# The down stage of a hybrid layer: two pairs interleaved product by product in each chunk, six weight parts split ahead, larger activation loads, and row sums spread over four blocks

## The chip, the core and the metric

The kernel runs on one core of a Trainium2 chip. The core has five engines with an instruction queue each: TensorE (PE in the profile; its weight loads are listed apart as PEld), VectorE (DVE), ScalarE (ACT), GpSimd (POOL) and SyncE (SP), which here only issues transfers. ACT also issues some. An engine runs its queue in order, so an instruction that waits holds up all that stands behind it. The metric is the device time of one execution in microseconds (us), the median over runs. A change of 0.2%, or 5 us, is about what a measurement of this kernel can tell from none.

## What is computed

One layer of a streaming encoder over 17 tiles of 128 rows (16 tiles of a prompt, one of samples), width 1024, in float32. It begins with a norm, an input projection, a gated delta rule beside a short convolution, and an output projection; the change leaves these alone. The second half, which it touches, is the feed-forward part:

```python
    h = rmsnorm(x, norm_ffn_pre)
    f = (jax.nn.silu(h @ w_gate) * (h @ w_up)) @ w_down
    x = x + rmsnorm(f, norm_ffn_post)
```

`w_gate` and `w_up` are 1024 x 2816, `w_down` is 2816 x 1024. The last line is the last norm; its result is the output `out_y`.

## The kernel before, in words

**Split products.** Each float32 factor is split into a high part (a cast by ACT) and the rest (a subtraction on VectorE or GpSimd), and a product is three matmuls: high x high, high x low, low x high. So each operand of a matmul costs a cast and a subtraction first, and a matmul that finds its operand not yet split waits. Around these stand forms with seven products in the place of eight: sums of blocks of the factors are formed first ("parts"), and the seven results are added into four sums.

**Gate and up stage (1123 to 2025 us).** The 17 tiles form three groups of 6, 6 and 5 tiles (`FGROUPS`). Each group goes through 22 blocks f of 128 columns (the matmuls of L1268, seven products per block, in `gate_up`). Of group 0, a block takes 14.5 us. In a block ACT copies PSUM banks out (L1300 to L1302), VectorE and GpSimd add them up, ACT applies SiLU (L1311, L1316), and VectorE multiplies. Next to that the weights of the next block are summed (`s` tiles sA to sD, L1234 to L1237) and split (L1243, L1244). Results are stored to DRAM in the layout in which the down stage reads them: `partd` for pairs of row blocks, `lastd` for the row block that is left single (stores L1332, L1340 and L1342, issued by ACT). At f = 16 of groups 0 and 1 the row sums of the next group are formed on VectorE: twelve subtractions, four each of L1166, L1167 and L1169 (`ffn_sums`).

**Down stage (2025.6 to 2492 us).** The 22 blocks form five chunks (`FCHUNKS`) of 4, 4, 4, 4 and 6 blocks. Per chunk there are c = 2 (in the last c = 3) slices q, and 7 x c weight parts, numbered (i, q); a part is a pair of 128 x 512 tiles `dw` (high and low), which `part` makes out of the rows that L1092 loads: a sum on VectorE for i = 1, 2, 3, 5 (L1099 to L1105), a cast on ACT (L1116) and a subtraction on VectorE or GpSimd (L1118). The parts live in a ring of 21 slots. Some slots reuse tiles of the stage before (sA and sB). `prep_step` makes the next part; five parts of the first chunk are made during blocks 11 to 15 of the last group, with the first two activation parts.

Eight pairs and one single run through every chunk. A pair is seven products with 3 x c matmuls of 128 x 512 each (L1434; 42 in a chunk with c = 2, 63 in the last); its seven activation parts are loaded by SP (L1424) in three loads of 2, 2 and 3 parts, and split by ACT (L1415) and VectorE or GpSimd (L1418, tile `as`). Four PSUM banks take the products of a pair; each is added into the accumulators `acc` by VectorE (L1393; in the first chunk ACT copies, L1467). Products 4 to 6 use banks that products 0 to 2 filled, so they wait until these were taken out. The pairs run one after the other, the single after the first pair (in the last chunk at the end). In the last chunk a pair ends with its last norm: two subtractions (L1493, L1494) and, for each of its two row blocks in `finish`, two squares on ACT (L1443), a sum (L1444), `f2m` on VectorE (L145), the power on GpSimd (L147), two products with `gpo` (L1447) and two multiply-adds (L1452) on VectorE, and two stores of `out_y`, one issued by ACT and one by SP.

**What sets the order.** The code names which engine does what; the order in which each engine's queue holds its instructions comes from a scheduler that simulates the program, within waits that the tiles' buffers and the `issue_after` marks set. So an edit can move instructions that it does not name, and the order is shown below where it matters.

## Time and profile before

| | us |
|---|---|
| median of 3 runs | 2511.01 |
| lowest and highest run | 2507.51, 2511.68 |
| profiled execution, its own time | 2506.84 |
| span in its trace | 2505.1 |
| TensorE busy, of the span | 2455.0 |
| end of the gate and up stage, begin of the down stage | 2025.6 |
| last matmul ends | 2492.5 |

The last two rows are from the timeline. Between span and time of the profiled execution lie 1.7 us. A row of the profile's groups reads: line, engine, operation, output <- inputs (names of tiles), shapes, count | busy us, mean ns of one | idle time before, and what ended it. A row of the waits reads: engine, what it was to write, line <- whom it waited for: us in all, times, longest. In the table by windows each engine has its busy time and in brackets the number of instructions, then the granted TensorE clock, and the share of the DMA engines and GB/s. A timeline row is: start, duration, engine, line, operation; a row with xN covers N instructions.

### The profile page before, as it was taken

Reading aid. Unit: us, or ns where it says so; the run is one execution under the profiler, and the core shown is the slowest. Engines: PE = TensorE matmul, PEld = TensorE weight load, DVE = VectorE, ACT = ScalarE, POOL = GpSimd, SP = SyncE. Lnnn points to the kernel's source line nnn. Section 1 sums busy time; section 2 is a strip of 40 time slices with the busy share of each in tenths; the row PEclk is TensorE's granted clock in tenths of the full one; section 3 lists DMA queues with packets and bytes.
Section 4 is the critical chain, followed back from the end, with each engine's and each line's share of the span. In section 5 each row is a group of like instructions: output and inputs, shape, how many; then the busy total and the mean of one; then the engine's idle time right before and its main releaser. Section 6 shows DMA issues by size and latency. Waiting matters only on the chain. (4 is left out here: it accounts for less than half of the span.)

```text
span 2505.1 us, 39369 instructions
## 1 busy us (share of the span) xinstructions
PE 2455.0 (98%) x14366; PEld 2247.2 (90%) x14366; DVE 1610.7 (64%) x3032; ACT 1059.6 (42%) x2355; POOL 579.5 (23%) x656
## 2 busy tenths in 40 slices
PE   8999999999999999999999999999999999999997
PEld 7898888889999988889999999999999987887786
DVE  5976645645656555878888754455555564677698
ACT  5556445445435343444443422223333345333343
POOL 1101011011011001135665400000000055455563
PEclk9999999999999999999999999999999999999999
DMA  7855555456667556688876878778898843333365
GB/s 275 310 213 193 211 198 193 175 170 231 242 225 240 200 183 211 209 297 319 292 269 238 290 250 277 264 242 267 291 308 280 259 147 122 93 126 126 128 224 184
DMA packets 282499, 561.91 MB, mean 224 GB/s; under 512 B 26109, under 2 KB 174785, under 8 KB 265025
## 3 DMA queue, kind: packets, MB, share of 16 engines
q1 hardware_dynamic: 161200, 483.52, 56.1%
q10 hardware_dynamic: 121104, 75.88, 9.7%
q8 instruction: 113, 1.85, 0.3%
q14 instruction: 82, 0.66, 0.1%
HBM read 400.62 MB, written 158.70 MB: 223 GB/s over the span
## 5 line engine op out<-in xcount | busy, mean ns | idle before, releaser
L1268 PE MATMUL fbank<-xh,fw 128*128 128x384 f32 (+1 forms) x3696 | 897.8, 326 | 5.9 <-ACT m L1300 2.6
L298 PE MATMUL dbank<-hi,w 128*128 128x384 f32 (+1 forms) x2240 | 672.0, 368 | 8.8 <-ACT w L277 6.2
L1268 PEld LDWEIGHTS fbank<-xh,fw 128*128 128x128 f32 x3696 | 651.0, 188 | 7.5 <-ACT m L1300 3.0
L1268 PE MATMUL fbank<-xl,fw 128*128 128x384 f32 (+1 forms) x1848 | 601.9, 326 | 0.0
L298 PEld LDWEIGHTS dbank<-hi,w 128*128 128x128 f32 x2240 | 416.8, 190 | 47.8 <-ACT w L277 6.2
L1434 PE MATMUL fbank<-dw,as 128*128 128x512 f32 x1884 | 442.6, 393 | 7.5 <-DVE as L1418 2.6
L1434 PEld LDWEIGHTS fbank<-dw,as 128*128 128x128 f32 x1884 | 353.6, 188 | 90.3 <-DVE acc L1393 3.9
L298 PE MATMUL dbank<-lo,w 128*128 128x384 f32 (+1 forms) x1120 | 402.3, 359 | 1.1 <-DVE lo L216 1.1
L1268 PEld LDWEIGHTS fbank<-xl,fw 128*128 128x128 f32 x1848 | 346.9, 188 | 0.0
L1418 POOL TENSOR_TENSOR as<-ar,as 128x256 fp32r<-128x256 f32 (+1 forms) x207 | 186.8, 913 | 226.3 <-ACT as L1415 223.8
L298 PEld LDWEIGHTS dbank<-lo,w 128*128 128x128 f32 x1120 | 212.9, 190 | 18.7 <-DVE lo L216 1.7
L1393 DVE TENSOR_TENSOR acc<-acc,fbank 128x512 f32<-128x512 f32 x248 | 166.3, 682 | 96.1 <-PE fbank L1434 81.9
L1415 ACT CAST as<-ar 128x256 fp32r<-128x256 f32 (+1 forms) x288 | 118.5, 428 | 184.6 <-PE fbank L1434 133.9
L1118 POOL TENSOR_TENSOR dw<-dr,dw 128x512 fp32r<-128x512 f32 x48 | 70.0, 1467 | 520.3 <-ACT dw L1116 520.3
L1243 ACT CAST fw<-rg 128x512 fp32r<-128x512 f32 x124 | 77.4, 624 | 193.8 <-PE fbank L1268 153.1
L302 DVE SCALAR_TENSOR_TENSOR acc<-R,cw,acc 128x384 f32<-128x384 f32 (+2 forms) x180 | 121.6, 678 | 53.2 <-ACT acc L332 44.2
L1313 DVE TENSOR_TENSOR c<-u,fbank 128x384 f32<-128x384 f32 (+1 forms) x66 | 34.9, 529 | 109.9 <-PE fbank L1268 109.9
L1311 ACT ACTIVATE m<-fbank 128x384 f32<-128x384 f32 (+1 forms) x66 | 31.3, 474 | 124.4 <-PE fbank L1268 117.3
L1309 DVE TENSOR_TENSOR m<-m,m 128x384 f32<-128x384 f32 (+1 forms) x44 | 23.1, 525 | 88.8 <-ACT m L1302 88.7
L1244 POOL TENSOR_TENSOR fw<-rg,fw 128x512 fp32r<-128x512 f32 x44 | 71.0, 1614 | 37.0 <-ACT fw L1243 34.7
L324 POOL COPY hist<-R 128x3 f32<-128x3 f32 x60 | 17.0, 283 | 254.5 <-ACT R L307 201.9
L1302 ACT COPY m<-fbank 128x384 f32<-128x384 f32 (+1 forms) x66 | 30.6, 463 | 82.9 <-PE fbank L1268 57.8
(362 smaller groups left out, 3550.6 us busy)
## 6 DMA issues: line engine op xcount, KB each, us to landing
w<-wsplit SPq DMA_DIRECT2D x105, 1024.0 KB, 5.1
fw<-fsplit SPq DMA_DIRECT2D x188, 512.0 KB, 4.7
fsplit<-fw SPq DMA_DIRECT2D x94, 512.0 KB, 3.9
partd<-pt ACTq DMA_DIRECT2D x88, 384.0 KB, 6.6
rg<-in_w_gu SPq DMA_DIRECT2D x62, 512.0 KB, 3.8
wsplit<-w SPq DMA_DIRECT2D x28, 1024.0 KB, 4.9
ar<-partd SPq DMA_DIRECT2D x48, 384.0 KB, 3.3
wr<-in_w_in SPq DMA_DIRECT2D x34, 512.0 KB, 5.8
```

Source lines behind the costliest of these rows:

```text
L298: T.matmul(ps[:, :c], l[:, k, :], r[k][:, :c], start=(k == 0 and r is hi and l is wh), stop=(k == KD - 1 and l is wl))
L302: r = V.scalar_tensor_tensor(acc, raw(d), w[:, d:d + 1], acc, op0=ALU.mult, op1=ALU.add)
L1118: e.tensor_tensor(out=w[1], in0=v, in1=w[0].bitcast(F32), op=ALU.subtract)
L1243: A.copy(w[:, 0], v)
L1244: e.tensor_tensor(out=w[:, 1], in0=v, in1=w[:, 0].bitcast(F32), op=ALU.subtract)
L1268: T.matmul(ps, w_[:, c], b_[k][:, :hw], start=(first and k == 0 and ci == 0), stop=(k == KH - 1 and ci == 2), skip_group_check=not first)
L1311: A.activation(sg0, b1, AF.Silu)
L1313: V.tensor_add(c21, u2, b3)
L1393: V.tensor_add(dst, dst, ps)
L1415: ins = A.copy(a[:, 0, :n], v)
L1418: e.tensor_tensor(out=a[:, 1, :n], in0=v, in1=a[:, 0, :n].bitcast(F32), op=ALU.subtract)
L1434: T.matmul(ps, a[:, x_, q * P:(q + 1) * P], w[y_], start=(start and q == 0 and ci == 0), stop=(q == c - 1 and ci == 2), skip_group_check=True)
```

## The change

Its parts, in the order of the kernel:

1. In `ffn_sums` the twelve subtractions are no longer formed at f = 16 together, but three per block at f = 16, 17, 18 and 19. For group 0 the tiles T3 now live in the tiles sA to sD, all four of which lie in one pool.
2. Six weight parts of the first down chunk are made ahead in the place of five, in blocks 10 to 15; the sixth slot lies in sC and sD.
3. In every down chunk, pairs 0 and 1 run as a "duo": their products alternate (in the first chunk in the order A, A, B, B and then by turns, since A has two activation parts ready; afterwards A, B, A, B). A weight part is now used by two products in a row. The single runs after the duo. In the last chunk the last norms of both pairs follow the duo's last product.
4. For the duo, activation parts are loaded in larger pieces: parts 2 to 6 at once for the first pair of the first chunk, 0 to 3 and 4 to 6 for the others. In the first chunk all seven splits of the second pair are on VectorE (before: two of seven).
5. `gpo` is loaded at the third chunk in the code's order and no longer at the second. Both halves of `out_y` are stored by SP, apart from the last ones.
6. In the very last norm the products with `gpo` go into a tile of their own, `xm`, and stand in the code beside the squares; the two accumulators of the single are two tiles.

Line numbers of the changed kernel differ: L1435 is the matmul of the down stage, L1473 the copy out of the banks in the first chunk, L1446 the squares, L1448 and L1453 the products with `gpo`, L1449 the sum, L1458 the multiply-add, L1460 the store, L1510 and L1511 the two subtractions.

```diff
@@ -1106,10 +1106,10 @@
             m = n % NDW
-            if m == NDR:
-                w = [ks.tile([P, 512], F32R, tag=nm, name=nm) for nm in SUMS[:2]]
+            if NDR <= m < NDR + 2:
+                w = [ks.tile([P, 512], F32R, tag=nm, name=nm) for nm in SUMS[2 * (m - NDR):2 * (m - NDR) + 2]]
             else:
-                pool, b = (dr, NDR) if m < NDR else (da, NDQ) if m <= NDR + NDQ else (dn, NDW - NDR - 1 - NDQ)
+                pool, b = (dr, NDR) if m < NDR else (da, NDQ) if m < NDR + 2 + NDQ else (dn, NDW - NDR - 2 - NDQ)
@@ -1157,10 +1157,10 @@
 
-        def ffn_sums(gi, hs, fs):
+        def ffn_sums(gi, hs, fs, sums=None, ks=range(KH)):
             hw = len(FGROUPS[gi]) * P // 2
-            t3, t2 = [], []
-            for k in range(KH):
+            t3, t2 = sums or ([], [])
+            for k in ks:
@@ -1177,7 +1177,7 @@
                     if nm == "T3" and not sums:
-                        t3.append(fs.tile([P, HW], F32, tag="t3", name="ft3", bufs=KH)[:, :hw])
+                        t3.append(ks.tile([P, 512], F32R, tag=SUMS[k], name="ft3").bitcast(F32)[:, :hw])
@@ -1230,7 +1230,7 @@
                 wl[:] = [nc.sync.dma_start(out=ru, in_=w_gu[f, 1].rearrange("p k c -> p (k c)"))]
-                s = [(fe if q > 1 else ks).tile([P, 512], F32R, tag=nm, name=nm).bitcast(F32) for q, nm in enumerate(SUMS)]
+                s = [ks.tile([P, 512], F32R, tag=nm, name=nm).bitcast(F32) for nm in SUMS]
@@ -1358,9 +1358,9 @@
                             hs.append(next(hload))
-                    if f == NF - 6:
+                    if NF - 6 <= f < NF - 6 + KH:
                         with tc.issue_after(gmark["V"].ins):
-                            t3 = ffn_sums(gi + 1, hs, fd)
+                            t3 = ffn_sums(gi + 1, hs, fd, t3 if f > NF - 6 else None, [f - NF + 6])
@@ -1378,7 +1378,7 @@
                     prep_step(1)
-                elif 11 <= f < 12 + NDR:
+                elif 10 <= f < 12 + NDR:
@@ -1420,9 +1420,10 @@
             n = src.shape[-2] * P
-            a = da.tile([P, 4, MC * P // 2], F32, tag="ar", name="ar", bufs=3)
-            nc.sync.dma_start(out=a[:, :hi - lo, :n], in_=src[:, lo:hi].rearrange("p i q c -> p i (q c)"))
-            return [a[:, i, :n] for i in range(hi - lo)]
+            a = da.tile([P, 4 * MC * P // 2], F32, tag="ar", name="ar", bufs=3)
+            a = a[:, :(hi - lo) * n].rearrange("p (i c) -> p i c", c=n)
+            nc.sync.dma_start(out=a, in_=src[:, lo:hi].rearrange("p i q c -> p i (q c)"))
+            return [a[:, i] for i in range(hi - lo)]
@@ -1435,23 +1436,28 @@
         def finish(v, places, tail=False, hold=False):
+            m = dr.tile([P, D], F32, tag="dr", name="xm", bufs=4).rearrange("p (h c) -> p h c", h=2) if tail else None
+            m = [m[:, h] for h in range(2)] if tail else v
...
             for h in range(2):
-                A.activation(junk, v[:, h], AF.Square, accum_out=ss[:, h:h + 1])
+                A.activation(junk, v[h], AF.Square, accum_out=ss[:, h:h + 1])
+                if tail:
+                    ins = V.tensor_mul(m[h], v[h], gpo[:, 512 * h:512 * h + 512])
...
             r = rstd(dn, ss[:, 0:1], 1, 1.0 / D, EPS, "f3" if tail else "f2")
-            for h in range(2):
-                ins = V.tensor_mul(v[:, h], v[:, h], gpo[:, 512 * h:512 * h + 512])
+            if not tail:
+                for h in range(2):
+                    ins = V.tensor_mul(v[h], v[h], gpo[:, 512 * h:512 * h + 512])
...
                 with tc.issue_after(ins.ins) if ins else ExitStack():
-                    ins = V.scalar_tensor_tensor(xt[:, c], v[:, h], r, xt[:, c], op0=ALU.mult, op1=ALU.add)
+                    ins = V.scalar_tensor_tensor(xt[:, c], m[h], r, xt[:, c], op0=ALU.mult, op1=ALU.add)
                 for p0, (r0, n) in places:
-                    (nc.sync if h else nc.scalar).dma_start(out=yr[r0:r0 + n, c], in_=xt[p0:p0 + n, c])
+                    (nc.scalar if (tail or hold) and not h else nc.sync).dma_start(out=yr[r0:r0 + n, c], in_=xt[p0:p0 + n, c])
@@ -1473,35 +1479,47 @@
             src = partd[gi][ch][j]
+            duo = pairs.index(u) < 2
             ready = first_parts if (ch, u) == (0, pairs[0]) else []
-            parts = (ready or load_parts(src, 0, 2)) + load_parts(src, 2, 4) + load_parts(src, 4, 7)
+            if duo:
+                parts = ready + load_parts(src, len(ready), 7 if ready else 4)
+                yield
+            else:
+                parts = load_parts(src, 0, 2) + load_parts(src, 2, 4)
+            if u == pairs[1] and not ch or u != pairs[1] and ch or not duo:
+                parts += load_parts(src, 4, 7)
...
                                                (b1, False, a1), (b2, False, a2), (b3, False, a3))):
-                product(b, ch, ready[i] if i < len(ready) else split(parts[i], V if i in ((0,) if end else (0, 3)) else G, bool(ready)), i, mid)
+                if i == 3 and len(parts) == 4:
+                    parts += load_parts(src, 4, 7)
+                e = V if i in ((0,) if end else (0, 3)) or (duo and not ch and not ready) else G
+                product(b, ch, ready[i] if i < len(ready) else split(parts[i], e, duo and not ch), i, mid)
...
                     prep_step(c)
-            cast.clear()
+                if duo:
+                    yield
...
                 r1, r2 = rows(u)
-                finish(acc[u][:, 0:2], [(0, r1)])
-                finish(acc[u][:, 2:4], [(0, r2)], hold=last)
+                finish((a1, a3), [(0, r1)])
+                finish((a2, a4), [(0, r2)], hold=last)
+            yield
...
             if u not in acc:
-                acc[u] = dn.tile([P, 2, 512], F32, name="accs")
-            c1, c2 = acc[u][:, 0], acc[u][:, 1]
+                acc[u] = [dn.tile([P, 512], F32, name=f"accs{h}") for h in range(2)]
+            c1, c2 = acc[u]
@@ -1522,16 +1540,23 @@
             end = ch == len(FCHUNKS) - 1
-            if ch == 1:
+            if ch == 2:
...
             spare = 0 if end else NDW - 7 * (len(chunk) // 2) + 2
-            for k, u in enumerate(pairs):
-                down_pair(ch, u, k == len(pairs) - 1)
-                if k == 0 and not end:
-                    down_single(ch, single)
-                elif 2 <= k <= 6:
+            duo = [down_pair(ch, u, False) for u in pairs[:2]]
+            for i in (0, 1, 0, 0, 1, 1) + (0, 1) * 5 if not ch else (0, 1) * 8:
+                next(duo[i])
+            for d in duo:
+                next(d, None)
+            cast.clear()
+            if not end:
+                down_single(ch, single)
+            for k, u in enumerate(pairs[2:], 2):
+                for _ in down_pair(ch, u, k == len(pairs) - 1):
+                    pass
+                if k <= 6:
...
```

How it moves instructions. First, VectorE's queue at the end of block 16 of group 0 (`ft` and `fh` are row sums and rows of the next group, `pt` what is stored, `fw` a weight split, sD a weight sum; - is before, + after, other rows stand in both):

```order
-L1166 TENSOR_TENSOR ft_13832<-fh 128x384
-L1166 TENSOR_TENSOR ft_13837<-fh 128x384
-L1166 TENSOR_TENSOR ft_13842<-fh 128x384
 L1336 TENSOR_TENSOR pt<-a_13822,a_13823 128x384 [waits DMAHW4_49,DMAHW5_49,DMAHW2_49,DVE_49]
-L1167 TENSOR_TENSOR fh<-fh 128x384 [waits DVE_49] x4
+L1167 TENSOR_TENSOR fh<-fh 128x384 [waits DVE_49]
 L1169 TENSOR_TENSOR ft_13830<-fh 128x384 [waits DVE_49]
 L1244 TENSOR_TENSOR fw<-sD,fw 128x512 [waits DMAHW6_49,PE_49,Activation_49]
-L1169 TENSOR_TENSOR ft_13835<-fh 128x384 [waits DVE_49]
-L1169 TENSOR_TENSOR ft_13840<-fh 128x384 [waits DVE_49]
-L1169 TENSOR_TENSOR ft_13845<-fh 128x384 [waits DVE_49]
 L1237 TENSOR_TENSOR sD<-rg,sB 128x512 [waits DVE_49]
```

Of twelve subtractions that stood ahead of `sD<-rg,sB` and of the sums of block 17 behind it, three are left there (with one L1166 ahead of this piece); the other nine stand in three like groups in the next three blocks.

Second, ACT's queue where the down stage begins, before (`as` are activation parts, `dw` weight parts, the `partd` stores those of the last pair's rows):

```order
L1332 DMA lastd_132<-pt 128x64 [waits DMAHW1_49,DVE_49]
L1415 CAST as<-ar 128x256 [waits DMAHW6_49]
L1116 CAST dw<-dr 128x512
L1415 CAST as<-ar 128x256
L1116 CAST dw<-dr 128x512 [waits PE_49]
L1116 CAST dw<-dr 128x512
L1415 CAST as<-ar 128x256 [waits DMAHW7_49]
L1116 CAST dw<-dr 128x512 x2
L1415 CAST as<-ar 128x256 x2
L1340 DMA partd_4_127<-pt 128x6x128 [waits DMAHW2_49,DVE_49]
L1340 DMA partd_4_127<-pt 128x6x128 [waits DMAHW3_49]
```

and after:

```order
L1332 DMA lastd_132<-pt 128x64 [waits DMAHW1_49,DVE_49]
L1340 DMA partd_4_127<-pt 128x6x128 [waits DMAHW2_49,DVE_49]
L1340 DMA partd_4_127<-pt 128x6x128 [waits DMAHW3_49]
L1415 CAST as<-ar 128x256 [waits DMAHW7_49]
L1415 CAST as<-ar 128x256
L1415 CAST as<-ar 128x256 [waits DMAHW6_49]
L1415 CAST as<-ar 128x256 x2
L1116 CAST dw<-dr 128x512
L1116 CAST dw<-dr 128x512 [waits PE_49]
```

The two `partd` stores, which wait for VectorE, stood behind ten casts; now all casts of the down stage stand behind them.

Third, VectorE's queue in the last chunk where the first finished pair's last norm stands, before (`acc_0_20767` is pair 0, `acc_1_20912` is pair 1, both ahead of their end or past it; L1393 takes a bank out):

```order
L1393 TENSOR_TENSOR acc_1_20912<-acc_1_20912,fbank 128x512 [waits PE_49]
L1444 TENSOR_TENSOR fss_23876<-fss_23876 128x1 [waits Activation_49]
L1447 TENSOR_TENSOR acc_0_20767<-acc_0_20767,gpo 128x512 [waits DVE_49]
L145 TENSOR_SCALAR f2m<-fss_23876 128x1 [waits DVE_49]
L1393 TENSOR_TENSOR acc_1_20912<-acc_1_20912,fbank 128x512 [waits PE_49]
L1447 TENSOR_TENSOR acc_0_20767<-acc_0_20767,gpo 128x512 [waits Activation_49]
L1452 SCALAR_TENSOR_TENSOR xr<-acc_0_20767,f2r,xr 128x512 [waits DMAHW2_49,Pool_49]
L1452 SCALAR_TENSOR_TENSOR xr<-acc_0_20767,f2r,xr 128x512 [waits DVE_49]
L1444 TENSOR_TENSOR fss_23892<-fss_23892 128x1 [waits Activation_49]
L1447 TENSOR_TENSOR acc_0_20767<-acc_0_20767,gpo 128x512
L1393 TENSOR_TENSOR acc_1_20912<-acc_1_20912,fbank 128x512 [waits PE_49]
```

and after (`acc_0_20772` and `acc_1_20793` are the duo's pairs, `acc_2_20991` is pair 2, the first after the duo):

```order
L1393 TENSOR_TENSOR acc_2_20991<-acc_2_20991,fbank 128x512 [waits PE_49]
L1449 TENSOR_TENSOR fss_23978<-fss_23978 128x1 [waits Activation_49]
L1453 TENSOR_TENSOR acc_0_20772<-acc_0_20772,gpo 128x512
L1458 SCALAR_TENSOR_TENSOR xr<-acc_0_20772,f2r,xr 128x512 [waits DMAHW2_49,Pool_49]
L1458 SCALAR_TENSOR_TENSOR xr<-acc_0_20772,f2r,xr 128x512 [waits DVE_49]
L1453 TENSOR_TENSOR acc_1_20793<-acc_1_20793,gpo 128x512 [waits Activation_49]
L145 TENSOR_SCALAR f2m<-fss_23978 128x1 [waits DVE_49]
L1449 TENSOR_TENSOR fss_23996<-fss_23996 128x1 [waits Activation_49]
L1453 TENSOR_TENSOR acc_1_20793<-acc_1_20793,gpo 128x512
L1393 TENSOR_TENSOR acc_2_20991<-acc_2_20991,fbank 128x512 [waits PE_49]
L1418 TENSOR_TENSOR as<-ar,as 128x384 [waits DMAHW2_49,Activation_49]
```

Before, pair 0's norm stands between pair 1's bank takings, with three to five instructions of the norm from one to the next; after, both pairs' norms stand one behind the other beside pair 2, with eight instructions of norms between two of its bank takings.

## The prediction

> **What bounds the kernel now.** I read the page first: the busy times, then the chain that ended last.
>
> ```profile
> PE 2455.0 (98%) x14366; PEld 2247.2 (90%) x14366; DVE 1610.7 (64%) x3032; ACT 1059.6 (42%) x2355; POOL 579.5 (23%) x656
> PE 39%; DVE 2%; DMA 1%; issue 1%; POOL 1%; ACT 0%; DVEq 0%; POOLq 0%; ACTq 0%; SPq 0%
> ```
>
> TensorE is the bound. The change removes no matmul, so it can only win back time in which TensorE stands: at most 2505.1 - 2455.0 = 50 us, of which much lies in stages that it doesn't touch. The next view is therefore the waits of TensorE in the places that the change names. In order: blocks 16 and 17 of group 0 (1360 to 1400, two rows); the start of the down stage (2020 to 2050, three rows); around the starts of chunks 1, 2 and 3 (2100 to 2130, 2190 to 2215, 2280 to 2300, a row each); the start of the last chunk (2360 to 2380, two rows).
>
> ```profile
> PE fbank L1268 <- ACT m L1300: 2.6, 1, 2.6
> PE fbank L1268 <- ACT m L1302: 1.9, 1, 1.9
> PE fbank L1434 <- DVE as L1418: 2.6, 1, 2.6
> PE fbank L1434 <- POOL dw L1118: 0.6, 2, 0.4
> PE fbank L1434 <- DVE dw L1118: 0.2, 1, 0.2
> PE fbank L1434 <- DVE acc L1393: 1.1, 1, 1.1
> PE fbank L1434 <- DVE acc L1393: 0.7, 1, 0.7
> PE fbank L1434 <- DVE accs L1393: 0.5, 1, 0.5
> PE fbank L1434 <- ACT dw L1116: 1.4, 1, 1.4
> PE fbank L1434 <- DVE dw L1118: 0.2, 1, 0.2
> ```
>
> A wait leaves out the restart and a slower clock, so I price a place by the matmuls that a stretch lacks. By windows of one length (two blocks of group 0; then the down stage's first 28 us; then the last chunk):
>
> ```profile
> 1347.50:1362.00 14.50, 14.50 (x86) 14.50 (x84) 10.67 (x14) 4.94 (x11) 7.70 (x6) 1.00 0.81 278
> 1362.00:1376.50 14.50, 14.50 (x85) 14.50 (x85) 14.47 (x21) 5.64 (x12) 7.59 (x6) 1.00 0.50 166
> 1376.50:1391.00 14.50, 9.96 (x56) 9.32 (x55) 10.61 (x15) 5.31 (x11) 6.38 (x5) 1.00 0.79 259
> 2028.00:2042.00 14.00, 10.53 (x42) 6.99 (x41) 13.28 (x14) 9.50 (x22) 13.24 (x11) 1.00 0.54 165
> 2042.00:2056.00 14.00, 14.00 (x63) 11.43 (x62) 10.31 (x13) 9.49 (x21) 10.64 (x10) 1.00 0.59 215
> 2364.00:2378.00 14.00, 12.34 (x46) 9.28 (x45) 8.80 (x11) 5.05 (x10) 11.08 (x10) 0.88 0.61 217
> 2392.00:2490.00 98.00, 97.93 (x427) 79.54 (x426) 91.40 (x151) 37.95 (x97) 52.02 (x49) 1.00 0.68 220
> ```
>
> Block 17 holds 56 matmuls in the place of 86: 30 x 14.5 / 86 = 5.1 us. The down stage's start lacks 63 - 42 = 21 at 14 / 63 = 0.222 us: 4.7 us. The last chunk's start lacks 17: 3.8 us. Chunks 1 to 3 I leave at their waits, 1.1 + 0.7 + 0.5 = 2.3 us. Together 15.9 us are within the change's reach.
>
> **The spread row sums.** VectorE's timeline where the sums stand (start, duration):
>
> ```profile
> 1363.62 4.98 DVE L1166 TENSOR_TENSOR ft<-fh 128x384 f32<-128x384 f32 x4
> 1368.99 1.95 DVE L1167 TENSOR_TENSOR fh<-fh 128x384 f32<-128x384 f32 x4
> 1371.93 1.48 DVE L1169 TENSOR_TENSOR ft<-fh 128x384 f32<-128x384 f32 x3
> ```
>
> They fill some 9 us of 14.5, VectorE is busy for 14.47 there, its sums for ACT come late, ACT's copies of the banks (L1300, L1302) behind them too, and TensorE stands a block later. Spread, a block gets a quarter: 9 / 4 = 2.2 us, on top of the 10.7 of the block ahead: 12.9 of 14.5. The same burst is in group 1, where the waits show nothing, so nothing is won there. Term: -5.1, between -5.1 and -3 (where one of the four blocks is a block with little room). I take -4.9.
>
> **The start of the down stage.** Before, pair 0 needed 14 weight parts (5 ready) and 7 activation parts (2 ready) for its 42 matmuls, 42 x 0.222 = 9.3 us: 14 splits in 9.3 us, with VectorE and GpSimd full (13.28 and 13.24 of 14). The duo needs 8 + 12 = 20 splits in 18.7 us, 1.07 per us in the place of 1.5. That is why later waits should go. But one new wait is plain from ACT's queue: the two `partd` stores now stand ahead of all casts.
>
> ```profile
> 2028.37 0.91 DVE L1338 TENSOR_TENSOR pt<-pt 128x320 f32<-128x320 f32 x1
> 2029.32 0.38 ACTq L1340 DMA_DIRECT2D partd<-pt  x1
> 2029.73 0.56 ACTq L1340 DMA_DIRECT2D partd<-pt  x1
> 2029.87 0.40 ACT L1415 CAST as<-ar 128x256 fp32r<-128x256 f32 x1
> 2028.30 0.39 PE L1434 MATMUL fbank<-sA,as 128*128 128x512 f32 x1
> ```
>
> TensorE has two activation parts ready, 2 x 6 = 12 matmuls, up to 2028.3 (where the third part's first one stands now, the last row). The third part's cast can begin when the stores are issued: 2028.37 + 0.91 + 0.38 + 0.56 = 2030.2, plus 0.40 of its own: 2030.6. If L1338 takes 0.49, as its neighbours without GpSimd beside them, 2030.2. So TensorE stands for 1.9 to 2.3 us, at once and for certain, and behind it all the casts of the second pair are queued, which the low halves on VectorE wait for. I add 0.2 for later parts. Term: 4.7 - 2.3 = -2.4; ends: 0 (GpSimd's chain of subtractions doesn't keep up after all) and -2.8.
>
> Five splits are moved from GpSimd to VectorE. Their prices in the groups of 2025 to 2056 (first two rows), and in those of 2392 to 2490 (last row):
>
> ```profile
> L1418 DVE TENSOR_TENSOR as<-ar,as 128x256 fp32r<-128x256 f32 x6 | 5.1, 857 | 0.0
> L1418 POOL TENSOR_TENSOR as<-ar,as 128x256 fp32r<-128x256 f32 x10 | 9.5, 966 | 74.8 <-ACT as L1415 74.8
> L1418 DVE TENSOR_TENSOR as<-ar,as 128x384 fp32r<-128x384 f32 x7 | 3.8, 549 | 0.0
> ```
>
> On VectorE 256 columns take 857 ns while GpSimd is full, and 384 columns 549 ns where GpSimd is busy for 52 of 98 us: the two slow each other. The Trainium skill says so too ("GPSIMD Engine Reference", Specifications): GpSimd shares its interfaces to the memory with VectorE, and contends with VectorE instructions that have two inputs there. It speaks against the move: by it two queues that run at once are no better than one, and this term would be 0 in the place of -2.4. The rows agree as to the direction, but 857 against 549 x 256 / 384 = 366 ns is a factor of 2.3 at full overlap, and the number of splits per us falls by 1 - 1.07 / 1.5 = 29% whoever does them. I keep -2.4, and the case of 0 below.
>
> **Chunks 1 to 3.** The waits are for a bank that VectorE hadn't taken out (L1393) at the change of chunks, where it makes weight parts. In the duo seven products lie between the filling of a bank and its next use, before three. So 2.3 us should go; the larger loads (up to 512 KB for c = 2) have three buffers and are asked for a pair ahead. Ends: -2.3 and +2 (a load of 4 to 6 waits for its buffer; one of 384 KB lands 3.3 us after issue by the page). I take -2.1.
>
> **The start of the last chunk.** TensorE waits there for the third slice of part 1 and for its subtraction. In the duo a part is used for two products in a row, so the third slice of part 1 comes 12 matmuls later: 12 x 0.222 = 2.7 us against 1.4 + 0.2 of waiting. The wait goes. The rest of the 3.8 is the clock, by the granted clock in windows:
>
> ```profile
> 2030.00:2037.00 7.00, 3.81 (x13) 2.20 (x14) 7.00 (x6) 4.78 (x12) 7.00 (x6) 1.00 0.73 225
> 2370.20:2372.80 2.60, 0.94 (x4) 0.20 (x3) 2.57 (x4) 1.29 (x3) 0.62 (x1) 1.00 0.59 236
> 2373.70:2377.10 3.40, 3.40 (x10) 2.65 (x9) 3.40 (x4) 1.56 (x3) 3.38 (x3) 0.50 0.23 26
> ```
>
> After 1.7 us without work the clock is halved for 3.4 us, which costs 3.4 / 2 = 1.7; after 3.2 us without work in 2030 to 2037 it isn't. The Trainium skill ("TensorE: Matmul & The Clock Gate", Part 1) has the clock halved after an idle window of about 3.4 us. The trace differs: it happens after less, and not after more. So a stall of 2 us, like the new one, may cost 1.7 on top; that is in the range. Term: -3.5; ends -3.8 and -1.
>
> **The last norms in the last chunk.** Nothing is added, but pair 0's norm moves behind the duo. VectorE's groups of 2392 to 2490 give a norm's price:
>
> ```profile
> L1452 DVE SCALAR_TENSOR_TENSOR xr<-acc,f2r,xr 128x512 f32<-128x512 f32 x28 | 27.9, 1037 | 0.5
> L1447 DVE TENSOR_TENSOR acc<-acc,gpo 128x512 f32<-128x512 f32 x28 | 19.7, 704 | 4.1 <-ACT junkd L1443 4.1
> L1493 DVE TENSOR_TENSOR acc<-acc 128x512 f32<-128x512 f32 x7 | 6.2, 881 | 0.2
> L1494 DVE TENSOR_TENSOR acc<-acc 128x512 f32<-128x512 f32 x7 | 5.3, 763 | 0.2
> L1444 DVE TENSOR_TENSOR fss<-fss 128x1 f32<-128x1 f32 x14 | 3.8, 272 | 1.5 <-ACT junkd L1443 1.5
> ```
>
> (27.9 + 19.7 + 6.2 + 5.3 + 3.8) / 7 = 9.0 us for a pair. VectorE is busy for 91.4 of those 98 us, so 6.6 are free. Some 8 of pair 0's 9 us come in later, into 6.6 free ones that aren't all usable: 1.5 to 2 us stay over when the last matmul ends, and TensorE may wait for a bank (with two norms in a row, eight instructions of norms stand between two bank takings). Term: +2; ends 0 and +8.
>
> **The end.** After the last matmul the last norm goes one by one: square, square, sum, `gpo`, another pair's multiply-add, then `f3m`.
>
> ```profile
> 2496.11 0.68 DVE L1447 TENSOR_TENSOR accs<-accs,gpo 128x512 f32<-128x512 f32 x1
> 2497.37 0.14 DVE L145 TENSOR_SCALAR f3m<-fss 128x1 f32<-128x1 f32 x1
> ```
>
> `xm` takes 1.4 us (2 x 0.68) from between sum and `f3m`. But in the new queue a multiply-add of 0.74 now stands between the two bank takings of the single, and ACT takes the square of the later one first. What is gained behind is lost ahead: 0, ends -1.3 and +1.
>
> **Costed at nothing.** The sixth weight part (one cast and one subtraction, in a block of the last group, where TensorE's waits show nothing; if that room were gone, their 1 to 2 us), T3's place (it is read in the stage before), `gpo` (used in the last chunk alone) and the stores of `out_y` on SP (a load behind a store that waits for its multiply-add comes later by that wait, but is issued a pair ahead).
>
> **The sum.** -4.9 - 2.4 - 2.1 - 3.5 + 2 + 0 = -10.9. Against the profiled execution's 2506.84 that is 2495.9; the median of the runs shown is 4.2 higher, 2511.0, and the forecast is made for it: 2500.1, say 2500.
>
> **Rivals.** (1) Only the spread sums pay: at the down stage's start GpSimd and VectorE slow each other, the new wait for the stores takes what is left, and the last chunk gives back what its start wins: -5, 2506. For it: the 857 ns, and ACT's queue. Against: 29% fewer splits per us. (2) Slower: the last chunk becomes VectorE's. That is decided where its 91.4 busy us grow past 98, so at 7% more; the two subtractions have one shape and take 881 and 763 ns, the products 704, so a price does hang on what runs beside. With both norms in a row and each bank taking behind them, 91.4 + 8 and 15% more on the norms' 64 us (9.6) make 109 in 98: 11 more for the chunk, and with stalls after each of six pairs of 1 us and a halved clock in three of them (1.7) 22, against 12.9 won elsewhere: +9, 2520. Against it: the free time ahead, where VectorE is busy for 8.8 of 14 us. (3) The norms cost 6 to 8 and the rest goes as said: -6, 2505.
>
> **How the numbers follow.** Forecast 0.60 (its own range 2493 to 2505, by the ends of the terms and 4 us of difference between runs), rival 1 0.20, rival 3 0.10, rival 2 0.10. Faster by over 0.2% (under 2506): 0.60, half of rival 1 and most of rival 3, 0.78. Within: 0.12. Slower: 0.10. The range reaches from 2492 (the lowest run and most ends favourable) to 2508.
>
> **What would show it.** Right: VectorE at 12 to 13 us in each of four blocks and no wait on L1300 or L1302 near 1382; one wait of 2 us for a cast L1415 near 2028; none on banks at the chunks' starts; clock 1.00 near 2372; VectorE over 95% from 2400 on. Wrong: waits of TensorE on L1393 in pairs 2 to 4 of the last chunk, or more than the 12.6 us of now between the last matmul and the span's end.

## The result, and the profile after

Over 14 runs each the kernel went from a median of 2511.54 us to 2508.79; the ratio is 0.9991, interval 0.9983 to 0.9999. The forecast was 2500, some 11 us less than before; 2 to 3 came. The profiled execution took 2506.63 us with a span of 2504.8, so the traces show one execution each of 2505.1 and 2504.8.

The head of the page, kernel after:

```profile
PE 2456.5 (98%) x14366; PEld 2248.1 (90%) x14366; DVE 1606.9 (64%) x3037; ACT 1056.7 (42%) x2355; POOL 582.6 (23%) x651
```

TensorE is as busy as before and stands for 2504.8 - 2456.5 = 48.3 us, before for 50.1. From the timeline, by the first and last matmuls of each stage (us):

| | before | after | forecast of the difference | difference |
|---|---|---|---|---|
| ahead of the gate and up stage (not changed) | 1104.3 | 1104.7 | 0 | +0.4 |
| gate and up stage | 921.2 | 921.9 | -4.9 | +0.7 |
| first down chunk | 87.8 | 88.2 | -2.4 | +0.3 |
| chunks 1 to 3 | 250.9 | 250.6 | -2.1 | -0.3 |
| last chunk | 128.3 | 126.4 | -3.5 + 2 | -1.8 |
| after the last matmul | 12.5 | 13.0 | 0 | +0.5 |

The last chunk came out at the number worked out; the other gains did not come. The waits of TensorE after, in the places of the prediction (a block is named after what VectorE works on; TensorE is then one block on): blocks 16 and 17 (1360 to 1400), the passage to group 1 (1400 to 1450), the start of the down stage (2020 to 2060), 2060 to 2066, the stretches 2120 to 2210 and 2290 to 2380, and the last chunk from 2380 on.

```profile
PE fbank L1268 <- ACT m L1302: 1.4, 1, 1.4
PE fbank L1268 <- ACT m L1301: 1.7, 1, 1.7
PE fbank L1435 <- ACT as L1415: 1.9, 1, 1.9
PE fbank L1435 <- DVE acc L1393: 1.4, 1, 1.4
PE fbank L1435 <- DVE acc L1393: 0.2, 1, 0.2
PE fbank L1435 <- POOL as L1418: 0.8, 1, 0.8
PE fbank L1435 <- DVE acc L1393: 1.1, 1, 1.1
```

The old waits are gone from nearly all their places. In their stead stand others: behind ACT's copies near 1387 and 1445, behind the casts at the start of the down stage, behind a bank taking at 2063, behind GpSimd's splits in chunk 3, and behind a bank taking in the last chunk. Windows of group 0, after (blocks 16, 17 and the passage to group 1):

```profile
1362.00:1376.50 14.50, 14.50 (x86) 14.50 (x85) 13.68 (x17) 6.69 (x13) 9.52 (x7) 1.00 0.66 232
1376.50:1391.00 14.50, 13.11 (x76) 12.79 (x75) 12.35 (x18) 5.35 (x11) 6.13 (x5) 1.00 0.77 256
1434.50:1449.00 14.50, 12.76 (x74) 12.44 (x73) 14.40 (x30) 5.90 (x13) 5.80 (x1) 1.00 0.69 230
```

VectorE's load is spread, less evenly than forecast: in four windows from 1362 on it is busy for 13.68, 12.35, 12.64 and 10.20 us, where "12 to 13 us in each of four blocks" was expected. TensorE still lacks 10 and 12 matmuls.

Waits of single traces scatter: the stretch ahead of the gate and up stage, which no experiment edits, took 1102.4 to 1108.2 us in the traces of this study. So the experiments are read by named waits and by stages, and by the medians where a whole edit is priced. Four of them were executed once only (smaller loads, splits back on GpSimd, casts on VectorE, last chunk without the interleaving): of those the trace alone is read.

### The profile page after: what moved, and what is told of

It reads as the page before. It is cut to its first block, busy times and chain, and to the rows that moved or that the text cites. A ratio compares the mean times of both kernels' runs of the same rounds, so it can differ in the third digit from the quotient of the medians.

```text
span 2504.8 us, 39351 instructions
## 1 busy us (share of the span) xinstructions
PE 2456.5 (98%) x14366; PEld 2248.1 (90%) x14366; DVE 1606.9 (64%) x3037; ACT 1056.7 (42%) x2355; POOL 582.6 (23%) x651
## 4 chain that ended last, share of the span: by engine, by line
PE 81%; DVE 9%; DMA 3%; ACT 3%; issue 2%; POOL 1%; ACTq 0%; SPq 0%; DVEq 0%; POOLq 0%
PE fbank L1268 33%; PE dbank L298 21%; PE fbank L1435 12%; PE dbank L1034 4%; PE tbank L1034 4%; DVE acc L1393 1%; DVE acc L302 1%; DVE xr L1458 1%; PE tbank L343 1%; DVE w L278 1%; PE obank L694 1%; PE gbank L749 1%; PE gbank L702 1%; PE gbank L686 1%; DMA xt<-in_x 1%
## 5 line engine op out<-in xcount | busy, mean ns | idle before, releaser
L1435 PE MATMUL fbank<-dw,as 128*128 128x512 f32 x1782 | 420.8, 393 | 4.2 <-ACT as L1415 1.9
L1435 PEld LDWEIGHTS fbank<-dw,as 128*128 128x128 f32 x1782 | 334.3, 188 | 82.3 <-ACT as L1415 5.2
L1393 DVE TENSOR_TENSOR acc<-acc,fbank 128x512 f32<-128x512 f32 x248 | 164.9, 681 | 90.9 <-PE fbank L1435 73.6
L1302 ACT COPY m<-fbank 128x384 f32<-128x384 f32 (+1 forms) x66 | 30.5, 462 | 95.7 <-PE fbank L1268 71.8
```

The source lines that it names most:

```text
L1393: V.tensor_add(dst, dst, ps)
L1435: T.matmul(ps, a[:, x_, q * P:(q + 1) * P], w[y_], start=(start and q == 0 and ci == 0), stop=(q == c - 1 and ci == 2), skip_group_check=True)
```

## The experiments

### The row sums: spread alone

The kernel before, with only the hunks of `ffn_sums` and of its call:

```diff
-                    if f == NF - 6:
+                    if NF - 6 <= f < NF - 6 + KH:
```

> Kernel before with the spread row sums alone. Theory A (the sums now stand on VectorE ahead of the chain that ends in the partd stores of odd blocks, and ACT's copy L1302 stands behind these stores): TensorE loses 1.3 to 1.7 us near 1387 and 1.5 to 2 near 1445 in the place of 4.9 near 1382 and 1388, so the gate and up stage is 1 to 2 us shorter than before and the time 0.9992 to 0.9996. Theory B (the two new waits come from the rest of the change): no wait over 0.5 us in either place, 4.5 to 5 us shorter, 0.9980 to 0.9982.

Ratio 0.9994 (0.9984 to 1.0003). TensorE's waits over the whole gate and up stage (1135 to 2015) in the traces: before, three rows; the changed kernel, two rows; this one, three rows.

```profile
PE fbank L1268 <- ACT m L1300: 2.6, 1, 2.6
PE fbank L1268 <- ACT m L1302: 1.9, 1, 1.9
PE fbank L1268 <- ACT m L1301: 1.2, 1, 1.2
```

```profile
PE fbank L1268 <- ACT m L1301: 2.9, 2, 1.7
PE fbank L1268 <- ACT m L1302: 2.7, 2, 1.4
```

```profile
PE fbank L1268 <- ACT m L1301: 4.2, 2, 2.9
PE fbank L1268 <- ACT m L1302: 1.6, 1, 1.6
PE fbank L1268 <- ACT m L1300: 0.4, 1, 0.4
```

5.7, 5.6 and 6.2 us: the burst's waits are gone and as much has come up elsewhere, without the rest of the change. So theory B falls. Its stage took 924.3 us, of which some 1.7 (half of 3.4) are a halved clock behind its longest wait (0.50 from 1446.7 to 1450.0). With the spread and the stores on ACT, five traces in which at most the last block's stores of this stage were edited took 919.8 to 921.9 us; with the burst, the kernel before took 921.2. A gain of 1 us would hide in that, one of 4.9 would not. One wait, of 1.1 to 2.7 us near 1150 (block 1, where no row sums stand), is in all of these traces, the kernel before's too. What happens in an odd block shows the timeline of the changed kernel, VectorE and ACT, block 17:

```profile
1380.53 0.55 DVE L1166 TENSOR_TENSOR ft<-fh 128x384 f32<-128x384 f32 x1
1380.99 0.55 DVE L1335 TENSOR_TENSOR pt<-a,pt 128x384 f32<-128x384 f32 x1
1381.46 1.65 DVE L1167 TENSOR_TENSOR fh<-fh 128x384 f32<-128x384 f32 x1
1383.04 0.55 DVE L1337 TENSOR_TENSOR pt<-pt,a 128x384 f32<-128x384 f32 x1
1383.50 0.55 DVE L1169 TENSOR_TENSOR ft<-fh 128x384 f32<-128x384 f32 x1
1383.97 0.55 DVE L1338 TENSOR_TENSOR pt<-pt 128x384 f32<-128x384 f32 x1
...
1384.55 2.20 ACTq L1340 DMA_DIRECT2D partd<-pt  x3
1386.85 0.48 ACT L1302 COPY m<-fbank 128x384 f32<-128x384 f32 x1 [5.04 <-DVE u L1308]
```

The three sums (0.55 + 1.65 + 0.55 = 2.75 us) stand among the sums of `pt` (L1335, L1337, L1338). ACT's three stores of `pt` wait for the last of these and take 2.2 us to issue, and the copy L1302, for which TensorE waits, stands behind them on ACT. The time was spread over the blocks, but into a chain that has no room.

### The row sums in even blocks

Even blocks store no `pt`. The kernel before, with a quarter of the sums in each of the blocks 12, 14, 16 and 18:

```diff
-                    if f == NF - 6:
+                    if f in (12, 14, 16, 18):
                         with tc.issue_after(gmark["V"].ins):
-                            t3 = ffn_sums(gi + 1, hs, fd)
+                            t3 = ffn_sums(gi + 1, hs, fd, t3 if f > 12 else None, [(f - 12) // 2])
```

> Kernel before with the row sums spread over the even blocks 12, 14, 16 and 18, which store no rows. Theory A (what hurts is the place in odd blocks, ahead of the stores, not the work): neither wait, the gate and up stage 4 to 5 us shorter than before, 0.9980 to 0.9984. Theory C (VectorE is too full in any block of group 0 for 2 to 3 us more): waits of 1 to 2 us as in the changed kernel, only moved to other blocks, 0.999 to 1.000.

Ratio 1.0011 (1.0002 to 1.0021), so nothing won. The waits of the whole stage, in the trace of its fastest execution:

```profile
PE fbank L1268 <- ACT m L1302: 2.8, 2, 1.5
PE fbank L1268 <- ACT m L1301: 2.8, 2, 1.7
```

Two of them are again L1302 in the odd block behind (1354.9 and 1385.7). VectorE comes into the odd block late by what the even one added, so that its last sum and the stores are late all the same. In block 15 the three stores begin at 1351.61 and L1302 at 1354.41; in the kernel before it is 1349.92 and 1352.73, although TensorE began its block 16 there 0.9 us later (1341.72, here 1340.82). So the chain is 2.6 us later against TensorE, of which 1.5 show as a wait. Theory A had the place too narrow.

### The stores off ACT

If it is the stores that hold up ACT's copies, another queue must issue them. The changed kernel, with all stores of L1340 on SP:

```diff
-                    nc.scalar.dma_start(out=partd[gi][ch][j, :, 1:7, q, :], in_=pt[:, :, j * P:(j + 1) * P])
+                    nc.sync.dma_start(out=partd[gi][ch][j, :, 1:7, q, :], in_=pt[:, :, j * P:(j + 1) * P])
```

> Changed kernel with all stores of rows into partd by odd blocks (L1340) issued by SP, those of the last block among them. Theory A (in odd blocks ACT's copies of the banks stand behind these stores, which wait for VectorE's last sum): TensorE's waits on ACT m L1301 and L1302 in group 0 go from 1.3 + 1.5 + 1.6 + 1.9 us (changed kernel) to under 1 us together; the gate and up stage is 4 to 6 us shorter than the 921.9 of the changed kernel, time 0.996 to 0.998 of before. Rival F (VectorE itself is late in odd blocks, whoever issues): the waits stay within 1 us of what they were, time as with the stores of the last block alone, 0.999.

Ratio 0.9967 (0.9955 to 0.9979), median 2501.31. From 1135 to 2015 the trace lists no wait of TensorE at all, the stage takes 914.4 us (921.9 in the changed kernel), and block 17 is full, with VectorE at 13.71 us (first row). L1302 now runs 4.2 us ahead of the same block's stores (the other two):

```profile
1376.50:1391.00 14.50, 14.50 (x86) 14.50 (x85) 13.71 (x17) 5.62 (x12) 9.09 (x7) 1.00 0.79 273
1377.11 0.48 ACT L1302 COPY m<-fbank 128x384 f32<-128x384 f32 x1 [0.48 <-PE fbank L1268]
1381.28 1.90 SPq L1340 DMA_DIRECT2D partd<-pt  x3
```

So VectorE's load was never too much for the block; rival F falls. The wait near 1150 went too, so part of the 7.5 us was there to win before the change. The edit does two things that aren't told apart: ACT's copies no longer stand behind the stores, and the stores land sooner (median 4.5 us from issue, 6.6 in the changed kernel), which frees `pt` sooner. The same edit on the kernel before, whose burst stays:

> Kernel before, with all its stores of L1340 issued by SP and nothing else. If ACT's place behind these stores is the cause and the spreading of the sums adds nothing (theory A1): the gate and up stage falls from 921.2 to 914 to 916 us, time 0.997 to 0.9975 of before. If the burst is a cause of its own (theory A2): TensorE still waits 2.5 to 5 us near 1382 to 1392, the stage is 917 to 919 us, 0.998 to 0.999.

Ratio 0.9990 (0.9981 to 0.9999), stage 919.5 us, of which some 1.7 are a halved clock (0.50 from 1382.1 to 1385.5). One wait over 0.2 us is left in it, in the block behind the burst:

```profile
PE fbank L1268 <- ACT m L1300: 3.2, 1, 3.2
```

### Both, and the burst again

The first of two kernels has the edit of the stores and the one of the splits that is told below (pair 1's splits in the first chunk on GpSimd apart from two); the second has the same, but the row sums in one burst and the end of the kernel as before the change:

```diff
-                    if NF - 6 <= f < NF - 6 + KH:
+                    if f == NF - 6:
...
-            m = dr.tile([P, D], F32, tag="dr", name="xm", bufs=4).rearrange("p (h c) -> p h c", h=2) if tail else None
-            m = [m[:, h] for h in range(2)] if tail else v
+            m = v
```

> Changed kernel with all stores of L1340 on SP and pair 1's splits in the first chunk on GpSimd apart from two. If both edits add up: gate and up stage 914 to 915 us, first chunk 85.3 to 85.8, time 0.9955 to 0.9965 of before. If the first chunk's gain needs what the last block's stores free on SP, or takes GpSimd from the next stage: first chunk 87, 0.9967.

> The same with the row sums in one burst at block 16 again, and with the very last norm's products behind its squares and in place (no xm). Stage of gate and up: 914 to 915 if the spreading adds nothing once the stores are on SP (A1), 917 to 919 if the burst costs by itself (A2). After the last matmul: 12.5 us if xm and its order lengthen the end, 13 if it is something else.

The first: ratio 0.9955 (0.9942 to 0.9969), median 2500.93, stage 914.3 us; it is faster than both kernels. The second: 0.9971 (0.9960 to 0.9982), stage 917.5. So spreading the sums is worth 3.1 us of the stage by the traces (4.0 by the medians, with intervals that overlap), once the stores are out of ACT's way, and about nothing with them there (921.9 after against 921.2 before). A2 holds. The second's waits, in the blocks behind the burst:

```profile
PE fbank L1268 <- ACT m L1300: 1.8, 2, 1.3
PE fbank L1268 <- ACT m L1301: 0.2, 1, 0.2
```

### The changed kernel without the spread

The changed kernel, with the two hunks of the row sums taken back:

> Changed kernel with the row sums back in one burst at block 16. If the parts add up (theory A): the burst's 4.9 us near 1382 and 1388 return and the two waits near 1387 and 1445 go, so 1 to 2 us longer than the changed kernel, its down stage alike within 0.5 us: 0.9997 to 1.000 of before. If theory B holds, the waits near 1387 and 1445 stay and the time is 3.5 to 5 us over the changed kernel: 1.0005 to 1.001 of before.

Ratio 0.9999 (0.9991 to 1.0008), stage 922.1 us: as with the spread, with the burst's waits back (2.7 us near 1386). The first down chunk has the same waits as the changed kernel's (1.9 us at its start, then the halved clock, 1.4 at the 37th us), so there the two parts of the change don't touch each other. The last chunk took 127.8 us, 1.4 more, with 2.3 us of waits on bank takings in the place of 1.1; why isn't known.

### The start of the down stage: the two stores

The changed kernel, with only the last block's two stores on SP:

```diff
+                    st = nc.sync if (gi, f) == (len(FGROUPS) - 1, NF - 1) else nc.scalar
-                    nc.scalar.dma_start(out=partd[gi][ch][j, :, 1:7, q, :], in_=pt[:, :, j * P:(j + 1) * P])
+                    st.dma_start(out=partd[gi][ch][j, :, 1:7, q, :], in_=pt[:, :, j * P:(j + 1) * P])
```

> Changed kernel, but the two partd stores of the very last gate and up block are issued by SP, so that ACT's casts no longer stand behind them. Theory D (these stores are the whole of the new wait at the down stage's start, and this wait starts the halved clock): TensorE's wait there falls from 1.9 to 0.3 to 0.9 us, the clock stays at 1.00, and the wait of 1.4 near 2063 shrinks since GpSimd starts its chain earlier: first chunk 3 to 5 us shorter, 0.9970 to 0.9980 of before. Theory E (GpSimd and VectorE can't keep up with the duo anyway): the wait only moves by some us to another part, the first chunk at most 1.5 us shorter, 0.9985 to 0.9990.

Ratio 0.9992 (0.9984 to 1.0001), first chunk 87.3 us against 88.2. The wait of 1.9 us is gone, and the halved clock behind it, but two others appear, 14 and 18 us on (waits from 2023 to 2056), and the one near the 37th us stays (1.6 us, before this edit 1.4):

```profile
PE fbank L1436 <- ACT dw L1116: 0.9, 1, 0.9
PE fbank L1436 <- DVE as L1419: 0.5, 1, 0.5
```

Why the first of them appears, the timeline of VectorE and ACT shows:

```profile
2026.87 5.05 DVE L1419 TENSOR_TENSOR as<-ar,as 128x256 fp32r<-128x256 f32 x5
2031.84 1.78 DVE L1105 TENSOR_TENSOR dr<-dr 128x512 f32<-128x512 f32 x1
...
2034.69 1.78 DVE L1105 TENSOR_TENSOR dr<-dr 128x512 f32<-128x512 f32 x1
...
2036.51 0.62 ACT L1116 CAST dw<-dr 128x512 fp32r<-128x512 f32 x1 [2.23 <-DVE dr L1105]
```

Five activation splits of 1 us each keep VectorE from the two weight sums L1105. ACT's cast waits for the second, and TensorE, up to 2037.2, for the cast. Theory E, then, and with a name to test: the splits that the change moved to VectorE.

### The start of the down stage: the splits

The kernel of the experiment ahead, with pair 1's splits in the first chunk as everywhere else:

```diff
-                e = V if i in ((0,) if end else (0, 3)) or (duo and not ch and not ready) else G
+                e = V if i in ((0,) if end else (0, 3)) else G
```

> The kernel with the last block's stores on SP, and in the first chunk pair 1's splits on GpSimd apart from two (before the move all but two, with the move none). Theory K (VectorE is the bound there: five splits of 1 us each stand ahead of the weight sums L1105 for which ACT's cast and TensorE wait): the wait of 1.1 us on ACT dw near 2037 goes and L1105 begins 3 to 5 us earlier; first chunk 0.5 to 2 us shorter than 87.3. Rival L (both engines slow each other, so the place doesn't matter): TensorE waits for GpSimd's splits by as much, first chunk 87 to 88.

The first chunk takes 85.5 us, against 87.3; of the waits of its first 30 us one is left:

```profile
PE fbank L1436 <- DVE as L1419: 0.4, 1, 0.4
```

VectorE's timeline there:

```profile
2028.94 2.72 DVE L1419 TENSOR_TENSOR as<-ar,as 128x256 fp32r<-128x256 f32 x3
...
2033.29 1.78 DVE L1105 TENSOR_TENSOR dr<-dr 128x512 f32<-128x512 f32 x1
...
2036.18 1.29 DVE L1105 TENSOR_TENSOR dr<-dr 128x512 f32<-128x512 f32 x1
```

In this trace the down stage begins 2.1 us later than in the one before it, and the first L1105 stands 1.5 us later, so 0.6 us earlier from the stage's start; the second ends 1.1 us earlier, and the wait on its cast is gone. K's 3 to 5 us was too much, its 0.5 to 2 us of the chunk were right (1.8). Other traces repeat it: with the splits shared the first chunk took 85.3, 85.5 and 85.5 us in three later kernels, with them on VectorE and the stores on SP 87.3 in three. Rival L falls: it matters which engine has the splits. That L1105 alone carries the gain isn't shown. Against the kernel before (87.8) the chunk is now 2.3 to 2.5 us shorter, about the term of the forecast.

### The larger loads

All activation loads in pieces of two parts, six buffers of half the size:

```diff
+            for l in range(lo, hi, 2):
+                h = min(l + 2, hi)
+                a = da.tile([P, 2 * MC * P // 2], F32, tag="ar", name="ar", bufs=6)
...
+                nc.sync.dma_start(out=a, in_=src[:, l:h].rearrange("p i q c -> p i (q c)"))
```

> The kernel with the last block's stores on SP, and all activation loads in pieces of two parts with six buffers of half the size. Theory G (in chunks 1 and 2 ACT waits for activation rows since the larger pieces hold their buffers longer): ACT's wait for ar in the first 25 us of chunk 1 falls from 5 us to under 2, and chunks 1 and 2 lose 0.3 to 0.8 us together. Theory H (the waits come from weight casts queued ahead of activation casts on ACT): chunks 1 to 3 stay within 0.3 us of 84.2, 83.0 and 84.7.

Chunks 1 to 3 took 83.8, 83.0 and 84.3 us (84.2, 83.0, 84.7). ACT's wait for activation rows in the first 25 us of chunk 1 fell from 8.1 us to 0.4, as theory G has it; the chunks gained 0.4 each at most, between G and H. So the larger loads make ACT wait, and TensorE loses little or nothing by it. The first chunk took 89.8, longer than with the larger loads (87.3), with a wait of 2.6 us near 2061 and some 1.7 us of halved clock (0.50) behind it.

### The casts on ACT in chunks 1 to 3

```diff
-            ins = A.copy(a[:, 0, :n], v)
+            ins = hi.tensor_copy(a[:, 0, :n], v) if hi else A.copy(a[:, 0, :n], v)
```

with `hi` VectorE for the duos of the chunks 1 to 3.

> The kernel with all L1340 stores on SP and pair 1's splits shared, and in the duos of chunks 1 to 3 the activation parts' casts (L1415) on VectorE in the place of ACT. Theory H (there the activation casts stand behind weight casts on ACT, which wait for w_dn rows and for VectorE's sums): TensorE's waits on splits L1418 near the 12th us of chunks 1 to 3, 0.9 + 0.3 + 0.9 us, fall to under 0.6 together, chunks 1 to 3 (84.4, 82.9, 85.2) at 82.2 to 83.5 each where the clock isn't halved. Rival N (GpSimd's chain of subtractions is the limit): these waits stay within 0.3 us. Rival O (14 casts more make VectorE the limit): they turn into waits on L1393 of 1 us and more per chunk.

The three chunks took 89.6, 85.9 and 89.2 us, with TensorE waiting for VectorE's casts for 6.4 us together, up to 1.9 at a time, and a halved clock (0.50) in the first and the third. Rival O, though on another line than L1393: VectorE becomes the limit. Whether ACT's order (H) or GpSimd's chain (N) makes the small waits of these chunks, the run can't tell, since the new ones cover them. That stays open; it is a matter of about 2 us.

### The last chunk without the interleaving

The kernel with the last block's stores on SP, with `duo` only outside of the last chunk:

```diff
-            duo = pairs.index(u) < 2
+            duo = pairs.index(u) < 2 and not end
```

> The kernel with the last block's stores on SP, without the interleaving in the last chunk alone. If the interleaving is worth what the two profiles show (theory M): the start's waits of 1.6 + 0.5 us on weight parts return, with or without a halved clock (first 63 matmuls 16.5 to 18.3 us in the place of 14.3), the waits of 1.3 us on L1394 near the middle go; last chunk 127 to 128.1 us against 126.4. The end after the last matmul is 13.0 us if it is xm's order that lengthens it, 12.5 if it is the deferred norms.

The last chunk took 130.4 us, against 126.5 with the interleaving, 3.9 us more, and more than theory M allowed. TensorE's three longest waits from 2360 on:

```profile
PE fbank L1436 <- ACT dw L1116: 1.4, 1, 1.4
PE fbank L1436 <- DVE acc L1394: 1.1, 1, 1.1
PE fbank L1436 <- DVE as L1419: 0.4, 1, 0.4
```

The waits for weight parts are back, its first 63 matmuls take 16.7 us in the place of 14.3. The wait behind a bank taking didn't go, it only moved (to 2426), so theory M was right about the start and wrong about the middle: what follows the first 63 matmuls took 113.7 us without the interleaving, 112.2 with it, and 110.0 in the kernel before. The end after the last matmul took 13.3 us, so it isn't the deferred norms alone that lengthen it.

## Why the prediction was wrong

**What bounds it.** Right: TensorE, and where it waits. The prices of the old waits were right for the trace that they were read from. The error lies in taking an old wait as a gain without pricing what comes next on the same chain.

**The spread row sums: -4.9 forecast, about 0 measured.** This is the step that failed, nearly half of the sum. It was argued from room: "Spread, a block gets a quarter: 9 / 4 = 2.2 us, on top of the 10.7 of the block ahead: 12.9 of 14.5". But the 10.7 were the lighter of two windows that alternate (the one ahead, 1333 to 1347.5, has 12.75), and busy time doesn't say where in the block an instruction may stand. In an odd block the sums went between the sums of `pt`, ahead of stores on ACT that ACT's copies stand behind. With these stores on SP there is no wait in the whole stage, and the spread is worth 3.1 us: less than 4.9 even there. The prediction counted ACT's stores at the start of the down stage and overlooked the same ones in every odd block. A second chain of the same kind showed too: VectorE's first sum into `pt` waits until the last store has read it. That is L1336, in block 20, before (first row) and after; the wait near 1445 hangs on it, since ACT's L1301 there waits for VectorE's L1329, which came at 1444.38 in the place of 1441.33. With the stores on SP all waits of L1336 for stores come to 0.5 us, with them on ACT to 14.9.

```profile
1423.73 0.56 DVE L1336 TENSOR_TENSOR pt<-a,a 128x384 f32<-128x384 f32 x1 [1.29 <-DMA partd<-pt]
```

```profile
1427.62 0.56 DVE L1336 TENSOR_TENSOR pt<-a,a 128x384 f32<-128x384 f32 x1 [6.15 <-DMA partd<-pt]
```

**The start of the down stage: -2.4 forecast, +0.3 measured.** The new wait was named and sized well (1.9 us, forecast 1.9 to 2.3). What was put into the range and not into the sum is the clock behind it, halved as in the last chunk before: the window after the wait shows 0.62, of which 3.4 us at 0.5, for 1.4 to 1.7 us.

```profile
2031.30:2035.80 4.50, 4.37 (x12) 3.46 (x13) 3.66 (x6) 3.93 (x11) 3.33 (x3) 0.62 0.54 160
```

And "I add 0.2 for later parts" was 1.4: the wait at 2063, where VectorE still does weight sums ahead of a bank taking. The argument by rate (1.07 splits per us in the place of 1.5) was about the sum over the engines; the splits that were moved to VectorE cost 1.8 us of it, as the experiment on them shows. With them back and the two stores on SP, the term's 2.4 us came. The rule of the Trainium skill that was weighed and set aside ("GPSIMD Engine Reference", Specifications) has GpSimd and VectorE contend for shared interfaces to the memory; by it this term was to be 0. The trace agrees as to the contention: a split on VectorE took 1.01 us beside a busy GpSimd (the five at 2026.87) and 0.42 where GpSimd stood (2045.02, both in the trace with the last block's stores on SP). But what decided was the balance, since it did matter which engine had the splits; that the term came out near 0 was luck for the rule.

**Chunks 1 to 3: -2.1 forecast, -0.3 measured.** The old waits on bank takings went, as said (1.1, 0.7 and 0.5 down to 0.2), and a wait on splits came, 0.8 in chunk 3. The step that failed is "So 2.3 us should go": it took a wait removed for time won. That the duo's need for two pairs' splits beside the same weight parts makes the new waits is an argument, not shown. Only 1.3 of the 2.3 us of waits went, and of these 1.0 came back as small delays between matmuls; traces of the same down stage differ by as much (250.6 and 251.2, with the last block's stores on SP 251.8 to 252.5). The larger loads cost 0.4 us a chunk at most.

**The start of the last chunk: -3.5 forecast.** Right: no wait, clock 1.00, and the first 63 matmuls go from 18.25 us to 14.30, -3.95. Without the interleaving the waits are back. But 1.6 of the 3.95 are the halved clock, which the trace before happened to have: two other traces of the same code (row sums spread alone, and in even blocks) wait as long and run at full clock, and there the 63 matmuls take 16.69. So the interleaving is worth 2.4 us at the start in an execution without the drop and 3.9 in one with it.

**The last norms: +2 forecast.** Right in size: the last chunk changes by -1.83, so the rest of it by -1.83 + 3.95 = +2.1. VectorE is full where that was said, and TensorE waits for it near 2452:

```profile
2400.00:2455.00 55.00, 53.92 (x234) 43.23 (x233) 54.01 (x86) 20.29 (x52) 33.91 (x30) 1.00 0.76 243
```

The cause is not the one given, or not alone: without the interleaving in the last chunk, so with pair 0's norm back in its place, there is a like wait of 1.1 us and the rest of the chunk is 113.7 us long, 3.7 over the kernel before. Something else of the change lengthens it (the stores of `out_y` on SP and the tiles changed there too; neither was tried alone). That +2 came is in part luck. Rival 2, VectorE as the bound, didn't come.

**The end: 0 forecast, +0.5 measured.** `xm` didn't shorten the chain. From the end of the two multiply-adds (2493.01 after, 2491.85 in the kernel with the end as before) to `f3m`:

```profile
2497.45 0.15 DVE L145 TENSOR_SCALAR f3m<-fss 128x1 f32<-128x1 f32 x1
```

```profile
2496.05 0.15 DVE L145 TENSOR_SCALAR f3m<-fss 128x1 f32<-128x1 f32 x1
```

(the changed kernel first, then the one with the end as before) it is 4.44 against 4.20 us, so `xm` costs 0.24, by the multiply-add between the two bank takings that the prediction named. The stretch after the last matmul is 13.0 us without `xm` too. Most of the 0.5 lies ahead of these stretches: the two multiply-adds end 1.20 us after the last matmul, in the kernel before 0.68 (2493.18 against 2492.50). So VectorE comes to the end with more left over, as "1.5 to 2 us stay over" had it in kind; what stands behind `f3m` is 0.3 shorter.

**The rivals.** What came is nearest to rival 1, turned about: the down stage's gains eaten as it says, by GpSimd and VectorE and the stores, while the last chunk kept 1.8 us; but the spread sums, which rival 1 kept, didn't pay.

## What to carry to other kernels

Before spreading work over blocks "with room", follow the chain that it is put into: here three short sums ahead of three stores on ACT's queue cost what the burst had cost, and moving the stores to another queue was worth 0.24%, some 6 us, by the two ratios (0.9991 and 0.9967, each against its own runs of the kernel before), more than the 4.9 us that the spread was to win. A transfer that waits for another engine belongs on a queue on which nothing that TensorE waits for stands behind it. And a removed wait counts as a gain only as far as the next one on the same engine lies behind it.

## What the runs showed of the hardware

The granted clock goes with much of the difference between runs of one kernel. Of 35 runs of the kernel before on one chip, the six with a mean clock of 0.996 took 2505.7 to 2509.5 us (mean 2508.1), the four with 0.992 took 2512.4 to 2515.6 (mean 2513.8): 5.7 us. Amid the matmuls the clock is halved for 3.4 us at a time, and whether a wait of some 2 us sets it off differs between executions of the same code: the first chunk's start of the kernel before has it in the spread-only trace (clock 0.50 from 2040.6 to 2044.0, behind a wait of 2.6 us) and not in its own, behind a like wait. The Trainium skill ("TensorE: Matmul & The Clock Gate", Part 1) has the drop after an idle window of about 3.4 us, and the return after about 3.4 us of sustained work. The traces differ as to the first: waits of 1.9 us were enough. (The 3.2 us without work in 2030 to 2037 that the prediction sets against this are three pieces, the longest of 2.6 us.) They agree as to the second: the halved stretches amid the matmuls are 3.4 us long.

A subtraction of two 512-wide rows on VectorE (L1105) took 1.78 us beside GpSimd's weight subtraction, in the first chunk, and 0.68 at 2296.5 of the changed kernel, beside GpSimd's activation splits: so it isn't GpSimd's being busy alone that slows it. Three stores of 384 KB took ACT 1.8 to 3.6 us to issue in the changed kernel (median 2.1); where they took 3.48 (from 1177.74) the copy L1302 behind them began at 1181.31, when they were issued, and TensorE waited 1.3 us for it.
